# Reciprocal roots of four RMS norms: a power on GpSimd in place of a square root on ACT and a Newton step on DVE

## The chip, the cores and the metric

The kernel runs on one core of a Trainium2 chip. TensorE multiplies matrices; ACT (ScalarE) evaluates functions and casts; DVE (VectorE) does elementwise work; GpSimd (POOL) is a further elementwise engine that here sets constants only; SyncE (SP) issues nearly all DMAs. Each engine works through its own queue in order, and semaphores join them. The metric is device time in microseconds (us), the median of several executions; a lower time is better.

## What is computed

One decoder layer over 512 positions of width 1024: attention and a gated recurrence side by side, then a feed-forward block with a causal convolution. It has four RMS norms, two before a block (pre) and two behind one (post):

```python
def rms_norm(x, g):
    xf = x.astype(jnp.float32)
    y = xf * lax.rsqrt(jnp.mean(xf * xf, axis=-1, keepdims=True) + RMS_EPS)
    return (y * g.astype(jnp.float32)).astype(x.dtype)
...
h = rms_norm(x, g_pre_mix[l])
proj = h @ w_in[l]
...
mix = jnp.concatenate([attn, lru], axis=-1) @ w_out[l]
x = x + rms_norm(mix, g_post_mix[l])
h = rms_norm(x, g_pre_ffn[l])
up = causal_dwconv(h @ w_up[l], w_conv_ffn[l], b_conv_ffn[l])
c_u, c_g = jnp.split(up, 2, axis=-1)
ffn = (jax.nn.gelu(c_g, approximate=True) * c_u) @ w_down[l]
x = x + rms_norm(ffn, g_post_ffn[l])
```

Each norm needs one reciprocal root for each position. With 512 positions on 128 partitions that is a column of 128 values four times per norm, 16 roots in all.

## The kernel before

Positions are cut into four tiles of 128 (t = 0 to 3). Every fp32 operand of a matmul is split into a high and a low part (`split`, lines 83 to 85: ACT casts the high part, line 84, and DVE subtracts it, line 85), and a product is three matmuls (`mm3`, lines 77 to 81). A framework orders the instructions of all engines by the program's order and their readiness, sets the semaphores, and gives the tiles of a pool their places one behind another.

The start: SyncE loads x and the first weights; for each tile `norm_transpose` (line 135) squares x on ACT with a running sum into `ss` (line 140), takes the root (`rstd_of`, line 121), multiplies x by root and weight on DVE (line 145, tile hn), transposes on TensorE (line 151, ptr) and splits the result into hT. The first projections (px, first for half the positions) need hT of tiles 0 and 1 and a split weight. Then come the small parameters of the recurrence (line 255 on, with an Exp on ACT in line 258 and a chain of small DVE instructions), the recurrence, attention, and the output projection.

The post norms are in `wide` (line 531), which makes 512 columns at a time (n = 0, 1) of the output projection and of the down projection: `weighted` (line 506) squares the PSUM bank on ACT with a running sum (line 510), and multiplies it by the weight on DVE (line 518). For n = 0 two small DVE instructions (line 513) turn the sum into the biases for the second half; for n = 1 the root is taken. `post_norm` (line 521) multiplies by the root and adds the residual (line 526). Behind the output projection the next pre norm follows tile by tile (`mixed`, line 561), and its transposed tiles h2T feed the up projection (pup). Behind the down projection the tiles go out by DMA (line 529).

One root (`rstd_of`) is five instructions: a square root on ACT (line 125), a scaled copy of the sum on DVE (line 126), a reciprocal (line 128) and a Newton step in two DVE instructions (lines 129 and 131). Line 119 takes a root of a constant at the very start, so that ACT loads the table for Sqrt early; a function whose table is not the loaded one costs a table load on ACT.

Lines 157, 159 and 575 allocate tiles that nothing uses (shift0, shift1, shift2); they move the tiles behind them in their pools. The second activation tile of the up projection lies in a pool at the other end of the memory.

Of the kernel before, what the change touches and what calls it, by code (L numbers as in the profile page):

```python
# [12 lines left out]
F32 = mybir.dt.float32  # L13
F32R = mybir.dt.float32r
BF16 = mybir.dt.bfloat16
AF = mybir.ActivationFunctionType
ALU = mybir.AluOpType

P = 128
S = 512  # L20
D = 1024
# [15 lines left out]
EPS = 1e-6  # L37
# [15 lines left out]
def hybrid_layer(  # L53
# [6 lines left out]
    nc = tc.nc  # L60
# [3 lines left out]
    cp = ctx.enter_context(tc.tile_pool(name="cp", bufs=1))  # L64
# [5 lines left out]
    def bank(name, tag):  # L70
        return ps.tile([P, 512], F32, tag=tag, name=name, bufs=BANKS[tag])
# [11 lines left out]
    def split(h, l, src, sub=None):  # L83
        nc.scalar.copy(h, src)  # L84
        (sub or nc.vector).tensor_sub(l, src, f32(h))  # L85
# [16 lines left out]
    xres = cp.tile([P, NT, D], F32, name="xres")  # L102
# [8 lines left out]

    consts = cp.tile([P, 2], F32, name="consts")
    nc.vector.memset(consts[:, 0:1], EPS)
    nc.vector.memset(consts[:, 1:2], -EPS / 2)

    root = cp.tile([P, 1], F32, name="root")
    nc.scalar.activation(root, consts[:, 0:1], AF.Sqrt)

    def rstd_of(ss, first, name):


        v = cp.tile([P, 5], F32, tag="rs", name=name, bufs=8)
        nc.scalar.activation(v[:, 0:1], ss, AF.Sqrt, scale=1.0 / D, bias=first[:, 0:1])
        nc.vector.tensor_scalar(
            v[:, 1:2], ss, -0.5 / D, first[:, 1:2], op0=ALU.mult, op1=ALU.add)
        nc.vector.reciprocal(v[:, 2:3], v[:, 0:1])
        nc.vector.scalar_tensor_tensor(
            v[:, 3:4], v[:, 2:3], v[:, 1:2], v[:, 2:3], op0=ALU.mult, op1=ALU.mult)  # L130
        nc.vector.scalar_tensor_tensor(
            v[:, 4:5], v[:, 3:4], 1.5, v[:, 2:3], op0=ALU.add, op1=ALU.mult)
        return v[:, 4:5]

    def norm_transpose(t, g, hT, pool):

        hn = pool.tile([P, D], F32, tag="hn", name="hn", bufs=4)
        sq = pool.tile([P, D], BF16, tag="sqn", name="sqn")
        ss = cp.tile([P, 1], F32, tag="ss", name="ss", bufs=8)
        nc.scalar.activation(sq, xres[:, t], AF.Square, accum_out=ss)  # L140
        r = rstd_of(ss, consts, "rpre")
        w = D // len(g)
        for n, gn in enumerate(g):
            hs = slice(n * w, (n + 1) * w)
            nc.vector.scalar_tensor_tensor(
                hn[:, hs], xres[:, t, hs], r, gn, op0=ALU.mult, op1=ALU.mult)
        for half in range(2):
            pt = bank("ptr", "tr")
            for j in range(4):
                k = 4 * half + j  # L150
                nc.tensor.transpose(pt[:, j * P:(j + 1) * P], hn[:, k * P:(k + 1) * P], ident)
            sl = (slice(None), slice(4 * half, 4 * half + 4), slice(t * P, (t + 1) * P))
            split(hT[0][sl], hT[1][sl], pt.rearrange("p (k q) -> p k q", q=P))
# [44 lines left out]
    for t in range(NT):  # L198
        norm_transpose(t, gpre, hT, pp)
# [7 lines left out]
    for r0, src in ((0, w_conv_lru[0]), (16, b_conv_lru), (20, b_r), (24, b_i), (28, lam)):  # L207
        v = src.rearrange("a (t c) -> (a t) c", c=P)
# [85 lines left out]
    def xr_block(t):  # L294
        return split_w(raw_xr[t // 2][:, :, (t % 2) * P:(t % 2 + 1) * P], KD, P), bank("px", "mm")

    first = [xr_block(t) for t in range(2)]
# [172 lines left out]
    for n in range(-LAG, len(tiles)):  # L470
        if 0 <= n + LAG < len(tiles):
            pr, s, i = tiles[n + LAG]
# [11 lines left out]
        pr, s, i = tiles[n]  # L484
# [21 lines left out]
    def weighted(pn, n, yg, g, ss):  # L506

        hs = slice(n * 512, (n + 1) * 512)
        sq = wp.tile([P, 512], BF16, tag="sq", name="sq", bufs=1)
        nc.scalar.activation(sq, pn, AF.Square, accum_out=ss[:, n:n + 1])  # L510
        if n == 0:
            for i, f in ((2, 1.0), (3, -0.5)):
                nc.vector.tensor_scalar(
                    ss[:, i:i + 1], ss[:, 0:1], f / D, f * EPS, op0=ALU.mult, op1=ALU.add)
            r = None
        else:
            r = rstd_of(ss[:, 1:2], ss[:, 2:4], "rpost")
        nc.vector.tensor_mul(yg[:, hs], pn, g[:, hs])
        return r

# [10 lines left out]
    def wide(src, x_at, ks, n, k_last, yg, g, ss, resident, done, held_split=None):  # L531


        tags = ("mm", "mm", "mm", "av") if n == 0 else ("sc", "sc", "mm", "mm")
        py = [bank(f"py{t}", tags[t]) for t in range(NT)]

        def units(k0, k1):
            raw = load_raw(src[k0 * P:k1 * P, n * 512:(n + 1) * 512], k1 - k0, 512)
            return [(u, split_w(raw[:, u - k0:u - k0 + 2], 2, 512)) for u in range(k0, k1, 2)]

        def mms(t, k0, w):
            for j in range(2):
                mm3(py[t], x_at(k0 + j, slice(t * P, (t + 1) * P)),
                    at(w, slice(None), j), k0 + j == ks[0][0], k0 + j == k_last)

        for k0, k1 in ks[:len(ks) - resident]:
            for u, w in units(k0, k1):
                for t in range(NT):
                    mms(t, u, w)
        held = [uw for k0, k1 in ks[len(ks) - resident:] for uw in units(k0, k1)]  # L550
        if held_split:
            held_split()
        for t in range(NT):
            for u, w in held:
                mms(t, u, w)
            r = weighted(py[t], n, yg[t], g, ss[t])
            done(t, r)
# [3 lines left out]
    def mixed(t, r):  # L561
        post_norm(yg[t], r, t, False)
        norm_transpose(t, (gpre2,), h2T, np_)

    yg = [np_.tile([P, D], F32, name=f"yg{t}") for t in range(NT)]
    ss = [cp.tile([P, 4], F32, tag="ss3", name="ss3", bufs=8) for t in range(NT)]
# [84 lines left out]
    ss = [cp.tile([P, 4], F32, tag="ss3", name="ss3", bufs=8) for t in range(NT)]  # L651
# [40 lines left out]
```

## Time and profile before

| | us |
|---|---|
| median of 3 executions | 589.58 (588.92 to 589.71) |
| the profiled execution | 590.37 |
| its span, first to last instruction | 588.5 |
| TensorE busy | 571.9 |
| DVE busy | 360.0 |
| ACT busy | 278.8 |
| GpSimd busy | 2.8 |

The page of the profile gives the busy time of each engine over the span, then the span in slices, the DMA queues, the chain of work that ended last, and the costliest groups of instructions. PE is TensorE, PEld its weight loads, PEclk the clock that it was granted, as a share of full speed. Where rows come from a list in order of time, they read: start in us, length in us, engine, line, operation, result<-operands, shapes, count, and in brackets how long the engine had stood idle before and who released it. Matmuls overlap, so their spacing is read from their starts.

### The profile page before, as it was taken

The numbers are of one execution on the slowest core, as the hardware profiler recorded it, in microseconds if no ns is written. First come the engines' busy times: TensorE is split into PE (matmuls) and PEld (weight loads), VectorE is DVE, ScalarE is ACT, GpSimd is POOL, SyncE is SP. The second block draws the span as 40 slices with busy tenths as digits, with TensorE's granted clock in tenths as the row PEclk, the third lists the DMA queues.
The fourth block names the chain that finished last, engine by engine and source line by source line (L and its number), as shares of the span: only waits on it lengthen the run. The fifth ranks groups of instructions, "written<-read, shape, count | busy, mean of one in ns | idle before, by whom it ended". The sixth has DMA issues, their size and how long they took to land.

```text
span 588.5 us, 6972 instructions
## 1 busy us (share of the span) xinstructions
PE 571.9 (97%) x2704; PEld 472.7 (80%) x2704; DVE 360.0 (61%) x664; ACT 278.8 (47%) x455; POOL 2.8 (0%) x10
## 2 busy tenths in 40 slices
PE   6989999999999999999999999999999999999995
PEld 3977888777788879988888888888888888888884
DVE  5869695788996896566656656656656521241225
ACT  7538954777775772534534434443444322132121
POOL 1000000000000000000000000000000000000000
PEclk9999999999999999999999999999999999999998
DMA  7562426233110634004403403413414223332103
GB/s 234 188 216 74 143 78 196 85 107 95 41 46 5 214 105 144 1 2 142 143 15 128 144 26 117 143 40 104 144 56 144 87 73 100 91 130 72 36 1 143
DMA packets 52265, 59.62 MB, mean 101 GB/s; under 512 B 2448, under 2 KB 41568, under 8 KB 52233
## 3 DMA queue, kind: packets, MB, share of 16 engines
q1 hardware_dynamic: 51201, 57.61, 30.5%
q10 hardware_dynamic: 1032, 1.57, 0.8%
q8 instruction: 21, 0.34, 0.2%
q14 instruction: 11, 0.09, 0.0%
HBM read 57.06 MB, written 3.69 MB: 103 GB/s over the span
## 4 chain that ended last, share of the span: by engine, by line
PE 88%; DVE 5%; ACT 3%; DMA 2%; issue 1%; DVEq 0%; SPq 0%
PE pup L80 14%; PE pup L81 14%; PE pup L79 14%; PE py L81 8%; PE py L80 8%; PE py L79 8%; PE pq L79 2%; PE pq L80 2%; PE pq L81 2%; PE pav L456 2%; DMA raw<-in_w_up_dram 2%; PE px L81 1%; PE px L79 1%; PE px L80 1%; PE ptp L446 1%; PE pv L80 1%
## 5 line engine op out<-in xcount | busy, mean ns | idle before, releaser
L85 DVE TENSOR_TENSOR wl<-raw,wh 128x1024 fp32r<-128x1024 f32 x82 | 100.1, 1221 | 125.2 <-ACT wh L84 124.5
L84 ACT CAST wh<-raw 128x1024 fp32r<-128x1024 f32 x82 | 85.6, 1048 | 144.0 <-PE py L81 72.2
L80 PE MATMUL pup<-h2Tl,wh 128*128 128x512 f32 x320 | 124.5, 389 | 0.0
L81 PE MATMUL pup<-h2Th,wl 128*128 128x512 f32 x320 | 124.5, 389 | 0.0
L79 PE MATMUL pup<-h2Th,wh 128*128 128x512 f32 x320 | 124.3, 389 | 0.0
L80 PEld LDWEIGHTS pup<-h2Tl,wh 128*128 128x128 f32 x320 | 60.1, 188 | 12.5
L81 PEld LDWEIGHTS pup<-h2Th,wl 128*128 128x128 f32 x320 | 60.1, 188 | 12.5
L79 PEld LDWEIGHTS pup<-h2Th,wh 128*128 128x128 f32 x320 | 60.0, 188 | 12.2
L79 PE MATMUL py<-wh,acth 128*128 128x512 f32 x176 | 68.9, 391 | 0.0
L81 PE MATMUL py<-wh,actl 128*128 128x512 f32 x176 | 68.8, 391 | 0.0
L80 PE MATMUL py<-wl,acth 128*128 128x512 f32 x176 | 68.8, 391 | 0.0
L80 PEld LDWEIGHTS py<-wl,acth 128*128 128x128 f32 x176 | 33.1, 188 | 7.2
L81 PEld LDWEIGHTS py<-wh,actl 128*128 128x128 f32 x176 | 33.1, 188 | 7.2
L79 PEld LDWEIGHTS py<-wh,acth 128*128 128x128 f32 x176 | 33.1, 188 | 7.1
L614 DVE SCALAR_TENSOR_TENSOR yu<-pup,par,yu 128x511 f32<-128x511 f32 (+1 forms) x44 | 33.0, 749 | 4.3 <-ACT yu L612 3.5
L621 ACT ACTIVATE yg<-yg 128x512 f32<-128x512 f32 x22 | 13.9, 632 | 44.9 <-DVE yg L614 44.9
L614 DVE SCALAR_TENSOR_TENSOR yg<-pup,par,yg 128x511 f32<-128x511 f32 (+1 forms) x44 | 32.8, 746 | 2.0 <-ACT yg L612 1.2
L622 DVE TENSOR_TENSOR yu<-yu,yg 128x512 f32<-128x512 f32 x22 | 15.2, 692 | 18.3 <-ACT yg L621 18.3
L81 PE MATMUL py<-wh,mixTl 128*128 128x512 f32 x64 | 25.4, 397 | 0.0
L79 PE MATMUL pq<-hTh,wh 128*128 128x512 f32 x64 | 25.4, 396 | 0.0
L81 PE MATMUL pq<-hTh,wl 128*128 128x512 f32 x64 | 25.3, 396 | 0.0
L79 PE MATMUL py<-wh,mixTh 128*128 128x512 f32 x64 | 25.2, 395 | 0.0
(196 smaller groups left out, 938.9 us busy)
## 6 DMA issues: line engine op xcount, KB each, us to landing
raw<-in_w_up_dram SPq DMA_DIRECT2D x22, 1024.0 KB, 5.1
raw<-in_w_down_dram SPq DMA_DIRECT2D x10, 1024.0 KB, 5.0
raw<-in_w_in_dram SPq DMA_DIRECT2D x5, 1024.0 KB
rawqk<-in_w_in_dram SPq DMA_DIRECT2D x8, 512.0 KB, 5.3
raw<-in_w_out_dram SPq DMA_DIRECT2D x4, 1024.0 KB, 5.1
xres<-in_x_dram SPq DMA_DIRECT2D x4, 512.0 KB, 5.6
out_dram<-yz SPq DMA_DIRECT2D x8, 256.0 KB, 2.0
toep<-fbd ACTq DMA_DIRECT2D x1, 1536.0 KB
```

Of the source, the lines that this page charges most:

```text
L79: nc.tensor.matmul(o, lh, rh, start=start, stop=False)
L80: nc.tensor.matmul(o, lh, rl, start=False, stop=False)
L81: nc.tensor.matmul(o, ll, rh, start=False, stop=stop)
L84: nc.scalar.copy(h, src)
L85: (sub or nc.vector).tensor_sub(l, src, f32(h))
L446: nc.tensor.transpose(ptr[:, j * P:(j + 1) * P], st[:, j * P:(j + 1) * P], ident)
L456: nc.tensor.matmul(pav[:, j * P:], vs, pT[i][:, j * S:j * (S - P) + S], start=j == 0 and i == 0, stop=j == NT - 1 and i == 1)
L614: nc.vector.scalar_tensor_tensor(y[:, d:], pt[:, :S - d], w_conv_f(2 - d, blk), y[:, d:], op0=ALU.mult, op1=ALU.add)
L621: nc.scalar.activation(yg, yg, AF.Gelu_apprx_tanh)
L622: nc.vector.tensor_mul(yu, yu, yg)
```

## The change

`rstd_of` takes the square root no more. The Square on ACT scales by D to the power -0.5, so that its running sum is the mean square at once; one DVE instruction adds epsilon (or, for a post norm, epsilon and the first half's mean), and GpSimd raises it to -0.5, which is a column of constants in the tile `power`. The tiles `consts` and `root` and the early square root go; the root's own tile shrinks from five columns to two; the two small instructions for n = 0 become one.

```diff
-    consts = cp.tile([P, 2], F32, name="consts")
-    nc.vector.memset(consts[:, 0:1], EPS)
-    nc.vector.memset(consts[:, 1:2], -EPS / 2)
-
-    root = cp.tile([P, 1], F32, name="root")
-    nc.scalar.activation(root, consts[:, 0:1], AF.Sqrt)
+    MEAN = D ** -0.5
+    power = cp.tile([P, 1], F32, name="power")
+    nc.vector.memset(power, -0.5)
 
     def rstd_of(ss, first, name):
-        v = cp.tile([P, 5], F32, tag="rs", name=name, bufs=8)
-        nc.scalar.activation(v[:, 0:1], ss, AF.Sqrt, scale=1.0 / D, bias=first[:, 0:1])
-        nc.vector.tensor_scalar(
-            v[:, 1:2], ss, -0.5 / D, first[:, 1:2], op0=ALU.mult, op1=ALU.add)
-        nc.vector.reciprocal(v[:, 2:3], v[:, 0:1])
-        nc.vector.scalar_tensor_tensor(
-            v[:, 3:4], v[:, 2:3], v[:, 1:2], v[:, 2:3], op0=ALU.mult, op1=ALU.mult)
-        nc.vector.scalar_tensor_tensor(
-            v[:, 4:5], v[:, 3:4], 1.5, v[:, 2:3], op0=ALU.add, op1=ALU.mult)
-        return v[:, 4:5]
+        v = cp.tile([P, 2], F32, tag="rs", name=name, bufs=8)
+        nc.vector.tensor_scalar(v[:, 0:1], ss, first, None, op0=ALU.add)
+        nc.gpsimd.tensor_tensor(v[:, 1:2], v[:, 0:1], power, op=ALU.pow)
+        return v[:, 1:2]
...
-        nc.scalar.activation(sq, xres[:, t], AF.Square, accum_out=ss)
-        r = rstd_of(ss, consts, "rpre")
+        nc.scalar.activation(sq, xres[:, t], AF.Square, scale=MEAN, accum_out=ss)
+        r = rstd_of(ss, EPS, "rpre")
...
-        nc.scalar.activation(sq, pn, AF.Square, accum_out=ss[:, n:n + 1])
+        nc.scalar.activation(sq, pn, AF.Square, scale=MEAN, accum_out=ss[:, n:n + 1])
         if n == 0:
-            for i, f in ((2, 1.0), (3, -0.5)):
-                nc.vector.tensor_scalar(
-                    ss[:, i:i + 1], ss[:, 0:1], f / D, f * EPS, op0=ALU.mult, op1=ALU.add)
+            nc.vector.tensor_scalar(ss[:, 2:3], ss[:, 0:1], EPS, None, op0=ALU.add)
             r = None
         else:
-            r = rstd_of(ss[:, 1:2], ss[:, 2:4], "rpost")
+            r = rstd_of(ss[:, 1:2], ss[:, 2:3], "rpost")
```

## Rows read from the trace of the kernel before

**Rows 1.** The page: the span, the busy time of each engine with its share and its instructions, and one of the three groups of matmuls of the up projection.

```profile
span 588.5 us, 6972 instructions
...
PE 571.9 (97%) x2704; PEld 472.7 (80%) x2704; DVE 360.0 (61%) x664; ACT 278.8 (47%) x455; POOL 2.8 (0%) x10
...
L80 PE MATMUL pup<-h2Tl,wh 128*128 128x512 f32 x320 | 124.5, 389 | 0.0
```

**Rows 2.** Busy time of each engine in stretches of the span: the stretch, its length, then busy us (instructions) of PE, PEld, DVE, ACT and POOL, the granted clock, the DMA share and GB/s. The row that begins with "sum" adds six stretches of 6 us from 198 to 234 us.

```profile
0.00:10.00 10.00, 5.69 (x12) 2.73 (x12) 4.12 (x15) 6.35 (x12) 1.74 (x8) 1.00 0.80 278
...
40.00:50.00 10.00, 7.96 (x34) 6.04 (x33) 6.57 (x10) 5.31 (x9) 0.00 (x0) 1.00 0.49 165
...
580.00:588.50 8.50, 1.92 (x9) 1.22 (x7) 3.95 (x9) 0.98 (x3) 0.00 (x0) 0.77 0.32 123
...
sum 36.00, PE 34.84 PEld 30.36 DVE 29.53 ACT 20.31 POOL 0.00; mean PE 5.81 PEld 5.06 DVE 4.92 ACT 3.39 POOL 0.00
```

**Rows 3.** The instructions that write or read the pre norms' root, by line: shortest, median and longest in ns, first and last start in us, shapes.

```profile
L126 DVE TENSOR_SCALAR rpre<-ss,consts x8: 206/211/215, 5.7 to 228.1; 128x1 f32<-128x1 f32 x8
L125 ACT ACTIVATE rpre<-ss,consts x8: 294/296/301, 5.7 to 228.1; 128x1 f32<-128x1 f32 x8
L128 DVE RECIPROCAL rpre<-rpre x8: 152/155/164, 6.1 to 228.4; 128x1 f32<-128x1 f32 x8
L129 DVE SCALAR_TENSOR_TENSOR rpre<-rpre x8: 210/220/221, 6.3 to 228.6; 128x1 f32<-128x1 f32 x8
L131 DVE SCALAR_TENSOR_TENSOR rpre<-rpre x8: 150/156/161, 6.5 to 228.8; 128x1 f32<-128x1 f32 x8
```

**Rows 4.** All engines in order of time at the start: the end of the first tile's Square, and what DVE does for tiles 0 and 1.

```profile
5.51 0.18 ACT L140 ACTIVATION_READ_ACCUMULATOR sqn<-xres 128x1 f32 x1
5.73 0.21 DVE L126 TENSOR_SCALAR rpre<-ss,consts 128x1 f32<-128x1 f32 x1 [4.68 <-ACT sqn L140]
...
6.77 1.41 DVE L145 SCALAR_TENSOR_TENSOR hn<-xres,rpre,gpre 128x512 f32<-128x512 f32 x2
...
8.86 0.75 DVE L145 SCALAR_TENSOR_TENSOR hn<-xres,rpre,gpre 128x512 f32<-128x512 f32 x1
```

**Rows 5.** The instructions on the sums of squares: the small DVE instruction with two constants.

```profile
L513 DVE TENSOR_SCALAR ss<-ss x16: 142/145/156, 189.6 to 522.4; 128x1 f32<-128x1 f32 x16
```

**Rows 6.** GpSimd in order of time, the whole span (four of nine rows, the last of them the last).

```profile
0.34 0.11 POOL L679 MEMSET const-uint8-127<- 128x1 uint8 x1
...
0.88 0.95 POOL L181 MEMSET graw<- 128x1024 f32 x1
1.86 0.29 POOL masks.py:199 TENSOR_SCALAR_AFFINE_SELECT ident<-ident 128x128 f32<-128x128 f32 x1
...
97.59 1.10 POOL L386 MEMSET klz<- 64x512 f32 x2 [95.30 <-DVE mixTl L85]
```

**Rows 7.** DVE's groups of one shape: line, result<-operands, shapes, count, busy us, mean ns, idle before. The pre-FFN norm's product by the root.

```profile
L145 DVE SCALAR_TENSOR_TENSOR hn<-xres,rpre,gpre_ffn 128x1024 f32<-128x1024 f32 x4 | 5.1, 1280 | 0.0
```

**Rows 8.** TensorE in order of time at the start: the first of the dense matmuls.

```profile
13.97 0.58 PE L81 MATMUL px<-hTh,wl 128*128 128x256 f32 x1 [0.27 <-DVE wl L85]
```

**Rows 9.** DVE, SyncE, ACT and TensorE in order of time between 25 and 44 us, one row each.

```profile
25.92 0.17 DVE L259 TENSOR_SCALAR sp<-sp 128x4 f32<-128x4 f32 x1 [0.74 <-ACT sp L258]
...
30.49 0.37 SPq L89 DMA_DIRECT2D raw<-in_w_in_dram  x1
...
41.47 1.04 ACT L84 CAST wh<-raw 128x1024 fp32r<-128x1024 f32 x1 [3.61 <-DMA raw<-in_w_in_dram]
...
43.13 0.70 PE L79 MATMUL pg<-xsh,gwh 128*128 128x512 f32 x2 [2.04 <-issue]
```

**Rows 10.** ACT's groups: the table loads, three of seven lines with eight loads in all (the others are lines 119 and 359, Sqrt; 363, Gelu; 437, Exp).

```profile
L125 ACT ACT_TABLE_LOAD x2 | 2.6, 1283 | 0.0
...
L258 ACT ACT_TABLE_LOAD x1 | 1.3, 1283 | 0.0
...
L621 ACT ACT_TABLE_LOAD x1 | 1.3, 1283 | 1.6 <-DVE yg L614 1.6
```

**Rows 11.** ACT and TensorE in order of time in the middle: the first post-mix root, and the up projection's wait for a transposed tile.

```profile
199.05 1.28 ACT L125 ACT_TABLE_LOAD   x1
200.34 0.30 ACT L125 ACTIVATE rpost<-ss 128x1 f32<-128x1 f32 x1
...
218.40 0.39 PE L80 MATMUL pup<-h2Tl,fw00h 128*128 128x256 f32 x1 [0.40 <-DVE h2Tl L85]
```

**Rows 12.** DVE in order of time at the end: the last tile's root.

```profile
582.68 0.21 DVE L126 TENSOR_SCALAR rpost<-ss 128x1 f32<-128x1 f32 x1 [1.40 <-ACT sq L510]
582.81 0.68 DVE L518 TENSOR_TENSOR yz<-py,gpost_ffn 128x512 f32<-128x512 f32 x1
...
584.04 1.41 DVE L526 SCALAR_TENSOR_TENSOR yz<-yz,rpost,xres 128x512 f32<-128x512 f32 x2
```

**Rows 13.** TensorE in order of time in the down projection, second half of its columns: the first and the last of eleven matmuls in a row that read the first activation tile, and of thirteen that read the second.

```profile
544.70 0.39 PE L80 MATMUL py<-wl,acth 128*128 128x512 f32 x1
...
546.97 0.39 PE L81 MATMUL py<-wh,actl 128*128 128x512 f32 x1
...
563.63 0.39 PE L79 MATMUL py<-wh,acth 128*128 128x512 f32 x1
...
566.42 0.39 PE L79 MATMUL py<-wh,acth 128*128 128x512 f32 x1
```

## Prediction

> **What bounds the kernel now.** I read the page's busy times first, then the busy times in stretches of 10 us, then the chain that ended last for the two ends, then the lists of instructions in order of time around the sixteen roots. TensorE is busy for 571.9 us of 588.5 [rows 1]; the changed work is on ACT and DVE, so it counts only where TensorE stands still. The stretches show where that is [rows 2]: 10 - 5.69 = 4.31 us in the first 10 us, 2.04 us between 40 and 50 us, 36 - 34.84 = 1.16 us between 198 and 234 us (the middle, where the post-mix and pre-FFN norms are), and 8.5 - 1.92 = 6.58 us at the end. In those four places I cost the change.
>
> **The price of a root.** Before, one root is a scaled add on DVE (211 ns) beside ACT's square root (296 ns), then reciprocal, product and sum on DVE (155, 220, 156 ns) [rows 3]. At the first tile the sum of squares is there at 5.51 + 0.18 = 5.69, DVE starts at 5.73 and the normalising product at 6.77: 1.04 us for the root, handover included [rows 4]. After, it is one add on DVE (145 ns with two constants, as line 513 shows [rows 5]; 211 ns with a column operand, as line 126 does [rows 3]), a handover, GpSimd's power, a handover. I call R the time from the add's end to the consumer's start. The trace holds no power. From below: GpSimd's 128x1 memset takes 0.11 us [rows 6] and ACT hands over in 0.04 us [rows 4], so 0.11 + 2 x 0.04 = 0.2 us. From above: its longest single instruction takes 0.95 us [rows 6], and DVE's longest product by a root 1.28 us [rows 7]; if the power is as long as the one and stands behind the other, R = 2.2 us. I take a power of 0.55 us, between the select (0.29 us) and that memset [rows 6], as a power is more than a compare but works on one element per partition; with 0.05 us for each handover R = 0.65 us. GpSimd's queue holds nothing between its constants of the first microseconds and a memset at 97.59 [rows 6], so no instruction is held up behind a power; on DVE whatever follows the consumer waits with it.
>
> **The start.** The chain that ended last enters TensorE's first dense matmuls at 13.97, and what releases them is DVE [rows 8]. First tile: 5.73 + 0.145 + 0.65 = 6.53 in place of 6.77, 0.24 us won. Second tile: DVE has 8.86 - 8.18 = 0.68 us between the two tiles' products, all root [rows 4]. If its add is issued ahead of the first product (1.41 us long), the power lies wholly beside it and 0.68 us are won; if behind, 0.145 + 0.65 = 0.80 us stand there and 0.12 us are lost. I take the middle, 0.28 us. Tiles three and four feed matmuls that come when TensorE is already busy, and I cost them at nothing: their cover is the dense matmuls from 13.97 on. Start: 0.24 + 0.28 = 0.52 us; with R = 0.2 us 0.69 + 0.68 = 1.37 us, with R = 2.2 us -1.31 and -1.67 us.
>
> **Does it get past 41 us?** TensorE waits there 2.04 us for a cast on ACT that stands behind another cast, which waits 3.61 us for a weight transfer; SyncE issued that at 30.49, when a DVE split had freed its buffer [rows 9]. So what is won at the start lasts only if that issue moves as well. It does, I think: the split follows the same chain, and ahead of it lies the Exp table load, 1.28 us on ACT [rows 10], for which DVE stands 0.74 us [rows 9]. With the square root of the start gone, the first table that ACT needs is one for Square, loaded while it waits for x. Square and Tanh run under Exp's table without a load of their own (no line but those of Exp, Sqrt and Gelu has one) [rows 10], so if that first table is Exp's, the later load goes. If not, it stays. Value: 0 to 1.28 us; I take DVE's own wait, 0.74 us. Start and Exp together move 43.13 by 0.52 + 0.74 = 1.26 us. The Trainium skill (ScalarE: Activation LUTs, What ACT_TABLE_LOAD costs) gives about 2.66 us for a change of table, 1.28 us of it the load and the rest a drain. The trace shows the load alone: at 199.05 it takes 1.28 us and the square root starts at 200.34 [rows 11]. By the page this term would be up to 2.66 us; the rows decide.
>
> **The middle.** Eight roots lie between 198 and 234 us, with one Sqrt table load at 199.05 [rows 11], which goes. Their ACT and DVE work runs mostly beside held matmuls, and only 1.16 us of TensorE can be won [rows 2], 0.40 us of it at 218.40, where the up projection waits for the second tile's transpose [rows 11]. The root alone is shorter by 1.04 - 0.80 = 0.24 us, two in a row per tile, and the load 1.28 us. I take 0.5 us of the 1.16. From below, a power that waits out a DVE product (1.28 us [rows 7]) in each of two roots would cost 2 x (1.28 - 0.24) = 2.1 us, less some slack: a loss of up to 1.5 us.
>
> **The end.** The last root is bare: DVE's scaled add starts at 582.68 and the final product at 584.04, but the multiplication by the weight lies between them (582.81 to 583.49) and must be done anyway [rows 12]. After: add until 582.89, power back at 582.89 + 0.65 = 583.54, so the product starts 0.50 us earlier. It can't win more than 584.04 - 583.49 = 0.55 us, and loses from R = 1.15 us on. The Sqrt load of this stage, one of the two on line 125 [rows 10], lies beside matmuls and brings nothing.
>
> **The sum.** 0.52 + 0.74 + 0.5 + 0.50 = 2.26, say 2.3 us. The profiled execution took 590.37 us (span 588.5 and 1.9 around it), so it would take 588.1 us; it stands 0.79 us above the median of the three runs, 589.58 us, so on the median's side the forecast is 587.3 us. All ends good: 1.37 + 1.28 + 1.16 + 0.55 = 4.4 us, 585.2 us.
>
> **Rivals.** (a) The power is long, and takes the place of what it removes. At R = 1.9 us the first tile loses 1.0 us; the second wins 0.2 us (add ahead) or loses 1.4 us (behind), so 0.6 us; Exp still gives 0.74 us; the middle loses 2 x (0.145 + 1.9 - 1.04) = 2.0 us in two roots, of which the table load's end takes up about half, 1.1 us are left; the end loses 582.89 + 1.9 - 584.04 = 0.75 us: 2.7 us slower, 592.3 us. It turns from gain to loss at R of about 1.3 us, and is a measurable loss from about 1.6 us. For it: a power is software on an engine that so far fills constants only. Against it: that engine's instructions of one column take 0.1 us [rows 6]. The SBUF — State Buffer page of the Trainium skill (Who interferes with whom) has a rule that would make R long in the middle: a DVE instruction with two SBUF inputs and a GpSimd instruction that reads SBUF exclude each other for the whole instruction. No trace here shows that, as GpSimd reads nothing beside DVE work; by that rule the middle loses and the end does not, since its multiplication takes one input from PSUM. (b) What is won at the start is given back at 41 us, since the transfer lands no earlier, and the middle stays hidden: the end alone is left, 0.5 us, 589.1 us. For it: the transfer shares the queues with others and takes 41.4 - 30.5 = 10.9 us [rows 9]. (c) The tiles move. Two small tiles go and one comes ahead of nearly all others in the pool, and the pads of lines 157, 159 and 575 stay. That a place can matter, the down projection shows: with weights from the first activation tile twelve matmuls' starts lie 0.227 us apart (546.97 - 544.70 over ten), with the second, at the other end of the memory, (566.42 - 563.63) / 12 = 0.2325 us [rows 13]. Should the 3 x 320 matmuls of the up projection [rows 1] fall to that, they cost 960 x 0.0055 = 5.3 us, which with the forecast's gain of 2.3 us makes 592.6 us. Should the second tile be cured, 192 matmuls give 1.1 us. Against it: operands move together, and no row has anything to say on the new place. (d) The Exp load stays: 588.0 us, inside the forecast's range.
>
> **How the numbers follow.** The forecast with (d), between 585.2 and 588.4 us: 0.50. Better still, with (c) to the good: 0.04. (b): 0.20. (a): 0.19. (c) to the bad: 0.07. From the 0.2% that a measurement of this kernel can tell from no change (588.4 to 590.8 us), faster has 0.53 (0.01 of the forecast ends short of it), same 0.23 (with the mild part of (a)), slower 0.24. The range reaches from all ends good, 585.2 us, to (a), 592.3 us; the bad end of (c), 592.6 us, is left out.
>
> **What would show it.** Right: a power under 0.7 us and its consumer within 0.8 us of the add; table loads down from eight to five; TensorE's first dense matmul at about 13.4; the stall near 41 us ending about 1.3 us sooner; the final product about 0.5 us behind the multiplication's old place, at 583.5 by the old clock. Wrong: DVE idle ahead of lines that use the root, released by GpSimd, for over 1 us; a stall at 41 us that has grown by what the start won; starts of 512-column matmuls over 0.23 us apart in the up projection.

## The result, and the profile after

The changed kernel is slower: 596.11 us (median of four, 595.38 to 597.41) against 589.64 us (588.92 to 590.03), a ratio of 1.0108 with a 95% interval of 1.0094 to 1.0121. Its profiled execution took 596.51 us with a span of 594.7 us, which is 6.2 us more than the span of before. The forecast was 2.3 us faster, with a range up to 592.3 us.

The changed program is some ten lines shorter: the power is line 122, its add line 121, the product by the root line 135, the transposes line 141. The page (answers to [rows 1]):

```profile
span 594.7 us, 6918 instructions
...
PE 575.5 (97%) x2704; PEld 475.4 (80%) x2704; DVE 353.1 (59%) x607; ACT 271.2 (46%) x435; POOL 13.4 (2%) x26
```

DVE has 6.9 us less to do and ACT 7.6 us less, as the change says. TensorE, with the same 2704 matmuls, is busy 3.6 us longer. Either it was slower or it was granted a lower clock. The busy times by stretch tell which (answer to [rows 2]; the columns are those of that group):

```profile
10.00:20.00 10.00, 7.40 (x32) 6.49 (x32) 8.07 (x13) 6.21 (x11) 1.46 (x1) 1.00 0.72 223
40.00:50.00 10.00, 8.95 (x26) 6.80 (x27) 5.88 (x8) 5.19 (x8) 0.00 (x0) 0.66 0.17 64
198.00:234.00 36.00, 34.15 (x194) 29.17 (x192) 30.05 (x42) 20.29 (x34) 5.30 (x8) 1.00 0.41 138
```

Between 40 and 50 us the granted clock is 0.66 where it was 1.00. In the trace's record of the clock it is at the lower of its two levels (1.2 GHz) from 41.8 to 48.6 us and then full (2.4 GHz) until 591.3; before, it was full from 18.0 to 584.6 without a break. (Ahead of the record's first entry, at 18.0 us before and 21.3 us after, the rows print 1.00, but 256-column matmuls start 0.21 us apart there and 0.12 us behind it.) Inside the fall, TensorE's 512-column matmuls start 0.43 us apart in place of 0.23 (TensorE in order of time, two rows):

```profile
43.89 0.63 PE L80 MATMUL pg<-xsl,gwh 128*128 128x512 f32 x1
44.32 0.63 PE L81 MATMUL pg<-xsh,gwl 128*128 128x512 f32 x1
```

In the middle TensorE is idle for 36 - 34.15 = 1.85 us, where it was 1.16.

What became of the roots: GpSimd in order of time, two of 16 powers, and DVE around the first tiles.

```profile
5.87 0.55 POOL L122 TENSOR_TENSOR rpre<-rpre,power 128x1 f32<-128x1 f32 x1 [3.72 <-DVE rpre L121]
...
16.47 1.46 POOL L122 TENSOR_TENSOR rpre<-rpre,power 128x1 f32<-128x1 f32 x1 [6.97 <-DVE rpre L121]
```

```profile
5.63 0.15 DVE L121 TENSOR_SCALAR rpre<-ss 128x1 f32<-128x1 f32 x1 [4.62 <-ACT sqn L130]
6.46 1.41 DVE L135 SCALAR_TENSOR_TENSOR hn<-xres,rpre,gpre 128x512 f32<-128x512 f32 x2 [0.67 <-POOL rpre L122]
...
8.72 0.15 DVE L121 TENSOR_SCALAR rpre<-ss 128x1 f32<-128x1 f32 x1 [0.80 <-ACT sqn L130]
8.80 1.40 DVE L135 SCALAR_TENSOR_TENSOR hn<-xres,rpre,gpre 128x512 f32<-128x512 f32 x2
```

The root is as priced: a power of 0.55 us, and 6.46 - 5.78 = 0.68 us from the add's end to the consumer. The first tile's product starts 0.31 us sooner than in [rows 4]. So the loss must lie elsewhere. TensorE's idle times from 10 us to the end of the start, all rows with a wait:

```profile
11.36 1.97 PE L141 MATMUL ptr<-ident,hn 128*128 128x128 f32 x8 [2.13 <-DVE hTl L85]
17.58 0.58 PE L81 MATMUL px<-hTh,wl 128*128 128x256 f32 x1 [1.10 <-DVE wl L85]
40.02 0.96 PE L79 MATMUL pv<-wh,hTh 128*128 128x512 f32 x3 [1.80 <-ACT wh L84]
42.47 1.19 PE L79 MATMUL pg<-xsh,gwh 128*128 128x512 f32 x2 [1.04 <-issue]
```

The matmul that stood at 13.97 in [rows 8] stands at 17.58, and it waits for wl, the first weight's low part, which has nothing to do with a root. DVE's and SyncE's order of time shows why, first in the kernel before, then in the changed one:

```profile
12.71 1.21 DVE L85 TENSOR_TENSOR wl<-raw,wh 128x1024 fp32r<-128x1024 f32 x1
...
15.27 1.23 DVE L85 TENSOR_TENSOR wl<-raw,wh 128x1024 fp32r<-128x1024 f32 x1
16.41 1.40 DVE L145 SCALAR_TENSOR_TENSOR hn<-xres,rpre,gpre 128x512 f32<-128x512 f32 x2
...
15.59 1.32 SPq L89 DMA_DIRECT2D raw<-in_w_in_dram  x2
```

```profile
11.81 0.73 DVE L135 SCALAR_TENSOR_TENSOR hn<-xres,rpre,gpre 128x512 f32<-128x512 f32 x1
...
13.73 0.74 DVE L135 SCALAR_TENSOR_TENSOR hn<-xres,rpre,gpre 128x512 f32<-128x512 f32 x1
...
16.31 1.21 DVE L85 TENSOR_TENSOR wl<-raw,wh 128x1024 fp32r<-128x1024 f32 x1
...
23.61 1.22 DVE L85 TENSOR_TENSOR wl<-raw,wh 128x1024 fp32r<-128x1024 f32 x1
```

```profile
14.62 0.42 SPq L89 DMA_DIRECT2D raw<-in_w_in_dram  x1
15.09 0.58 SPq L492 DMA_DIRECT2D gpost_mix<-in_g_post_mix_dram  x1
...
26.45 4.38 SPq L89 DMA_DIRECT2D raw<-in_w_in_dram  x2
```

In the kernel before, DVE did the two wl at 12.71 and 15.27 and the products of tile three at 16.41. Now tile three's two products (11.81, 13.73) and the first of its two splits (15.64) go ahead of both. The order on DVE is made when the program is built, by readiness, and with the changed instructions the framework put tile three first. The second wl frees a load buffer, and so SyncE's queue is in another order too: before, two weight loads went out together from 15.59 on, now gpost_mix stands between them and the second goes out at 26.45.

To place the loss, the start of the same matmuls in both traces:

| matmul | before, us | after, us | later by |
|---|---|---|---|
| first transpose | 7.67 | 7.26 | -0.41 |
| first on wl (px) | 13.97 | 17.58 | +3.61 |
| first of the value projection (pv) | 35.95 | 40.02 | +4.07 |
| first of the gate projection (pgr) | 71.32 | 77.19 | +5.87 |
| 33rd on a weight's low part, output projection | 192.87 | 198.77 | +5.90 |
| 21st on a streamed weight, up projection | 256.92 | 263.33 | +6.41 |
| first of the down projection | 460.92 | 467.33 | +6.41 |
| last of the down projection | 581.52 | 588.12 | +6.59 |
| end of the span | 588.5 | 594.7 | +6.2 |

Nearly all is lost ahead of 77 us, half a microsecond in the middle, and 0.4 us is won back at the end.

### The profile page after: what moved, and what is told of

Read it like the earlier page. It is cut to its first block, busy times and chain, and to the rows that moved or that the text cites. A ratio compares the mean times of both kernels' runs of the same rounds, so it can differ in the third digit from the quotient of the medians.

```text
span 594.7 us, 6918 instructions
## 1 busy us (share of the span) xinstructions
PE 575.5 (97%) x2704; PEld 475.4 (80%) x2704; DVE 353.1 (59%) x607; ACT 271.2 (46%) x435; POOL 13.4 (2%) x26
## 4 chain that ended last, share of the span: by engine, by line
PE 86%; DVE 5%; ACT 3%; DMA 3%; issue 1%; POOL 1%; SPq 0%; DVEq 0%; POOLq 0%; ACTq 0%
PE pup L79 13%; PE pup L80 13%; PE pup L81 13%; PE py L80 8%; PE py L79 8%; PE py L81 8%; PE pq L79 2%; PE pq L80 2%; PE pq L81 2%; PE pav L446 2%; PE px L81 1%; DMA raw<-in_w_up_dram 1%; PE px L80 1%; PE px L79 1%; PE ptp L436 1%; PE pv L79 1%
```

## Theories and experiments

Theory A: the order. The shorter roots let the framework put tiles three and four ahead of the first weight's split; TensorE starts late, stalls near 40 us and loses its clock there. Theory B: the power itself, its handovers or its memory port, holds the kernel up. Beside them stand the prediction's rivals, above all (c), moved tiles.

### 1. The first weight's split written ahead of tile three

```
     for t in range(NT):
+        if t == 2:
+            first.append(xr_block(0))
+        if t == 2:
+            first.append(xr_block(1))
         norm_transpose(t, gpre, hT, pp)
```

> The changed kernel with the split of the first weight's two halves written ahead of the normalising of tiles three and four, so that DVE does the first low part (wl) before the products of tile three. All 16 roots are still powers. Theory A (the order: the shorter roots let tiles three and four go ahead of the first weight's split, and TensorE's dense run starts 3.6 us late): the first matmul on wl at 13.0 to 14.0 us in place of 17.58, no fall of the granted clock near 42 us, 586.5 to 588.5 us. Theory B (the power itself, its wait or its port, costs the time): nothing is taken from the powers, so 594 to 597 us.

Measured: 591.34 us, ratio 1.0025 (1.0016 to 1.0035). All powers are there and 1.3 us of the 6.5 are left (the kernel before took 590.04 beside it); the clock is full from 17.4 to 587.4 us. The first matmul on wl came at 14.94, a little later than said, but the gate projection started at 71.03, 0.3 us ahead of before. What is missing lies in the middle (+0.56 us between the output projection's mark of the table and the up projection's) and in the other runs of this kernel, which took 0.3 to 1.8 us longer than the profiled one; what that spread comes from was not looked into. The time lies above theory A's range and below theory B's.

### 2 and 3. The power in one part only

The 16 roots are made by two functions, the power and the old one, and each call names which; the early square root stays. In the second run the power is at the start alone, in the third everywhere else.

```
-        r = rstd_of(ss, consts, "rpre")
+        r = rstd_of(ss, EPS, "rpre") if new else rstd_old(ss, consts, "rpre")
```

> The changed kernel with the power for the four roots at the start only; the 12 roots after the mixer and at the end are the old ones (square root on ACT, reciprocal and Newton step on DVE), with the early square root and the Exp table load that belong to them. With these instructions the framework puts the first wl ahead of the products of tile three again. Theory A: the start is not late although its roots are powers: 588.5 to 590 us, the first matmul on wl before 14.5 us. Theory B: the start's loss of 5.9 us is the powers' there, so 595 to 597 us.

Measured: 589.12 us, ratio 0.9987 (0.9975 to 0.9998): slightly faster than before, with all four powers at the start. The first matmul on wl, said to come before 14.5 us, comes at 16.46, and yet nothing is lost. The gate projection starts at 69.65, 1.7 us sooner, as the stall of [rows 9] is gone: SyncE's queue has another order here, with the load of gpre_ffn ahead of the weight's in place of behind it; the weight's load goes out at 29.22 and ACT has cast it by 39.4.

> The changed kernel with the power for the 12 roots after the mixer and at the end only; the four at the start are the old ones. Both theories: the start as in the kernel before. Theory A: the later part alone, +0.4 in the middle and -0.4 at the end, 589 to 590 us. Theory B with a cost for every power: 592 us or more. Rival C (moved addresses slow the second half's matmuls): the places of the tiles are the old ones here, so no step of TensorE's pace.

Measured: 589.71 us, ratio 1.0001 (0.9990 to 1.0011). The middle costs 0.64 us here, the end wins 0.4. The start is not quite as before, although up to 44 us its instructions stand in the same order on SyncE, DVE and TensorE (one root's instruction moved on ACT): the weight's load goes out 0.71 us sooner than in [rows 9] and is cast 1.47 us sooner, so that the stall near 41 us is 0.85 us and the gate projection starts at 69.94, 1.38 us ahead of before.

```profile
29.78 0.37 SPq L89 DMA_DIRECT2D raw<-in_w_in_dram  x1
...
40.00 1.05 ACT L84 CAST wh<-raw 128x1024 fp32r<-128x1024 f32 x1 [2.42 <-DMA raw<-in_w_in_dram]
```

The medians of the two kernels differ by 0.3 us. So a place behind 41 us in a single trace can be off by about a microsecond, and the medians decide.

### 4. The order of after, with no power at all

The kernel before, whose two first low parts are queued on DVE as in the changed kernel: the first behind tile three's first split (the expectation says tile four's), the second behind tile four's last. issue_after orders the issue and adds no wait; done_l holds the two splits of the tile just written. Lines are left out at the dots.

```
+        with tc.issue_after(ins.ins):
+            nc.vector.tensor_sub(l, src, f32(h))
...
+        if t >= 2:
+            first.append(xr_block(t - 2, done_l[t - 2]))
```

> The kernel before, with no power in it, whose first two low parts (wl) are queued on DVE behind the first and the last hTl of tile four (with the order of issue alone, no wait more), so that DVE's order at the start is that of the changed kernel. Theory A: the start's loss comes without any power: the first matmul on wl at 17 us or later, 593 to 597 us; if the granted clock falls again near 42 us it is the late start that brings it, if not, 592 to 593.5. Theory B: 589 to 590.5 us.

Measured: 597.21 us, ratio 1.0125 (1.0108 to 1.0143). The whole loss, and not one power. TensorE's waits for wl and for pv are those of the changed kernel, and the clock is at the lower level from 41.9 to 48.7 us. TensorE in order of time, two rows:

```profile
17.97 0.58 PE L81 MATMUL px<-hTh,wl 128*128 128x256 f32 x1 [0.98 <-DVE wl L97]
...
40.78 0.97 PE L79 MATMUL pv<-wh,hTh 128*128 128x512 f32 x3 [1.80 <-ACT wh L84]
```

This run and the ninth settle that the 6 us are the order's, and not the power's.

### 5. A product in the power's place

```
-        nc.gpsimd.tensor_tensor(v[:, 1:2], v[:, 0:1], power, op=ALU.pow)
+        nc.gpsimd.tensor_tensor(v[:, 1:2], v[:, 0:1], power, op=ALU.mult)
```

> The changed kernel with GpSimd's power made a product with the same two inputs (the roots are then not computed: each norm is scaled by -0.5 times the mean square). The order of all engines stays that of the changed kernel. Theory A (the order costs the time, the power's length does not): 594 to 597 us, the granted clock falls near 42 us again. Theory B (the power's length or its port): the loss shrinks with the product's shorter time, to 592 us or less.

Measured: 593.82 us, ratio 1.0059 (1.0043 to 1.0075), between the two ranges. The product takes 0.19 us where the power took 0.55. The clock falls again (40.6 to 47.4 us) and the gate projection is 5.04 us late, so the start's loss stays, as A says. But the middle turns from +0.51 us to -1.09 us. TensorE's waits there, first in the changed kernel, then in this run:

```profile
212.16 1.09 PE L141 MATMUL ptr<-ident,hn 128*128 128x128 f32 x8 [0.54 <-DVE hn L135]
219.03 1.06 PE L141 MATMUL ptr<-ident,hn 128*128 128x128 f32 x8 [0.53 <-DVE rpost L121]
225.53 1.06 PE L141 MATMUL ptr<-ident,hn 128*128 128x128 f32 x8 [0.69 <-DVE hn L135]
234.18 1.06 PE L141 MATMUL ptr<-ident,hn 128*128 128x128 f32 x8 [0.27 <-DVE hn L135]
```

```profile
211.06 1.09 PE L141 MATMUL ptr<-ident,hn 128*128 128x128 f32 x8 [0.26 <-DVE hn L135]
223.45 1.06 PE L141 MATMUL ptr<-ident,hn 128*128 128x128 f32 x8 [0.17 <-DVE hn L135]
```

The transposes of a normalised tile stand in TensorE's queue at the same places in both; 0.54 + 0.53 + 0.69 + 0.27 = 2.03 us of waiting became 0.43. There the power's length does count, because the transposes stand where with a GpSimd instruction of 0.2 us the tile would be almost ready. In the kernel before they stood further back (the first three 45 to 69 matmuls behind their tile's last one, now 32 or 33), and waited for nothing.

### 6 and 7. One late split at a time

The fourth run's edit for the first wl alone (behind tile three's first split, not tile four's as the expectation has it), and for the second alone.

> The kernel before with the first low part (wl) alone queued behind the first hTl of tile four; the second wl stays in its place behind it, and SP's queue keeps its order. It parts theory A in two. A1 (the dense run's late start itself costs the time): the first matmul on wl at 17 us or later and most of the 6 us lost, 593 us or more. A2 (the second wl matters, because it frees the raw buffer that SP's next weight load waits for, and a late load starves TensorE near 40 us, where the clock falls): the second weight load goes out before 22 us, no stall at 38 us and no fall of the clock, 589.5 to 592 us.

Measured: 592.34 us, ratio 1.0037 (1.0025 to 1.0050), between the two ranges. The first matmul on wl is at 17.82, TensorE's full clock begins at 23.7 in place of 18.0, and the gate projection is 1.93 us late. The clock doesn't fall later.

> The kernel before with the second low part (wl) alone queued behind the last hTl of tile four; the first wl stays early. SP's second weight load then goes out after the late wl, and the load of gpost_mix moves ahead of it. A1 (the dense run's late start costs the time): it starts at 14 us here, so 589 to 591.5 us. A2 (the late release of the raw buffer and the late load): the load goes out at 24 us or later, TensorE stalls near 38 to 40 us, the clock falls near 42 us, 593 to 597 us.

Measured: 589.64 us, ratio 0.9995 (0.9984 to 1.0005). The load went out at 24.23, and ACT cast it in time (SyncE and ACT in order of time, one row each):

```profile
24.23 0.38 SPq L89 DMA_DIRECT2D raw<-in_w_in_dram  x1
```

```profile
30.66 1.05 ACT L84 CAST wh<-raw 128x1024 fp32r<-128x1024 f32 x1 [2.33 <-DMA raw<-in_w_in_dram]
```

Run 7 shares with run 4 that the first two blocks are written earlier, so that alone costs nothing. And A2 is wrong: a late load alone starves nobody. A1 explains a third: the first wl late alone costs 2.5 us in the median (592.34 against 589.82), of the 7.2 us of run 4. The full loss needs both. With both, ACT's queue has the cast that pv needs behind a convolution start (xc) that waits for the last px matmul. ACT in the kernel before, where this cast is early, and in the changed kernel:

```profile
28.15 1.04 ACT L84 CAST wh<-raw 128x1024 fp32r<-128x1024 f32 x1
```

```profile
38.25 0.78 ACT L300 ACTIVATE xc<-px,par 128x512 f32<-128x512 f32 x1 [4.69 <-PE px L81]
38.93 2.93 ACT L84 CAST wh<-raw 128x1024 fp32r<-128x1024 f32 x3
```

### 8. Power at the start and at the end

> The changed kernel with the power at the start (four roots) and after the down-projection (four roots), and the old roots for the eight between. If the middle's roots lose 0.5 to 0.6 us by their place in TensorE's queue and the end's gain 0.4 us, it is the run with the power at the start alone less 0.4: 588.7 us, 0.9978 of the kernel before. Theory B (each power costs): above that run's 589.1 us.

Measured: 589.00 us, ratio 0.9978 (0.9968 to 0.9988). As said: faster than both kernels. The last matmul is 1.36 us ahead of before and the span 1.8 us shorter, so the end gives 0.4 us. Most of its lead comes, as in run 2, from the stall near 41 us, which is gone.

### 9. A useless square root

```
+    eps_t = cp.tile([P, 1], F32, name="eps_t")
+    nc.vector.memset(eps_t, EPS)
+    root = cp.tile([P, 1], F32, name="root")
+    nc.scalar.activation(root, eps_t, AF.Sqrt)
 
     MEAN = D ** -0.5
```

> The changed kernel, all 16 roots powers, with nothing added but the early square root on a constant that the kernel before had (its result is used by nobody). It brings a square-root table load and the Exp table load back: work that was removed. With these instructions the framework puts the first two wl ahead of the products of tile three again. Theory A (the order costs the time): 588.6 to 590.4 us, that is the run with the power at the start alone plus 0.6 for the middle, less 0.4 at the end; no fall of the clock near 42 us. Theory B: work added to the changed kernel makes it no faster, 596 to 598 us.

Measured: 589.43 us, ratio 0.9998 (0.9987 to 1.0009). Work that nobody uses, with a table load of 1.28 us that comes back, makes the changed kernel 6.7 us faster. DVE does the first split early again (the second at 16.82 is behind tile three's products, not ahead of them as said), and ACT has pv's cast at 29.33. TensorE has no idle time between 40 and 50 us, though much between 10 and 20 us:

```profile
11.19 1.23 DVE L85 TENSOR_TENSOR wl<-raw,wh 128x1024 fp32r<-128x1024 f32 x1 [1.32 <-ACT wh L84]
13.53 1.40 DVE L140 SCALAR_TENSOR_TENSOR hn<-xres,rpre,gpre 128x512 f32<-128x512 f32 x2
16.82 1.22 DVE L85 TENSOR_TENSOR wl<-raw,wh 128x1024 fp32r<-128x1024 f32 x1
...
29.33 1.05 ACT L84 CAST wh<-raw 128x1024 fp32r<-128x1024 f32 x1 [0.64 <-ACT wh L84]
```

```profile
10.00:20.00 10.00, 6.39 (x30) 5.77 (x31) 7.56 (x12) 7.20 (x11) 1.97 (x2) 1.00 0.66 161
...
40.00:50.00 10.00, 10.00 (x44) 8.00 (x44) 7.41 (x11) 5.99 (x10) 0.00 (x0) 1.00 0.47 165
```

One part of theory A does not hold. TensorE is idle for 3.61 us between 10 and 20 us here, against 2.60 in the changed kernel, and the first matmul on wl comes at 17.43, as late as there (17.58). The first pv matmul is 1.60 us later than before (37.55), but the gate projection is 0.71 us ahead: the stall near 41 us, 2.04 us before and none here, took up what the start lost. So a late first matmul on wl does not by itself cost the 6 us. The changed kernel differs from this run by the late second wl (23.61), pv's cast behind xc, the waits near 40 us and the clock's fall.

The four powers of the start are the same in both, and in run 2, so the shorter roots alone do not make the late order either. Which of the removed instructions tips it is not shown.

### 10 and 11. The middle's transposes further back

On top of run 9 the transposes are emitted apart from the norm, and those of the first two tiles are queued behind a later matmul of the output projection.

```
+                if t >= 2 and i == 2 and len(turns) > 0:
+                    turns.pop(0)(m)
```

The transposes go behind the matmul m; the eleventh run has `i == 1`.

> The run with the square root back, and in the middle the transposes of the first two tiles queued on TensorE nine and ten matmuls later (2.0 to 2.3 us), behind a named matmul of the out-projection. If the middle's loss is TensorE waiting for the products (0.5 to 0.8 us ahead of each of four groups of transposes) because they stand too early in its queue for a power of 0.55 us, the first two waits go: 1.0 to 1.6 us less than with the square root back alone, 587.4 to 589 us. If the loss is in the powers or in DVE, no change: 589 to 590 us.

Measured: 589.54 us, ratio 0.9993 (0.9983 to 1.0003), not below 589 us as said. The two waits went, but the up projection now waits 0.80 and 0.60 us for the tiles that were transposed later. The middle costs +0.33 us, as in run 9 (+0.39).

> As the run before it, with the transposes of the first two tiles only three and four matmuls later (0.7 and 0.9 us), just over the waits of 0.5 to 0.8 us that they are to cover. If those waits are all there is to gain, it comes out as with nine and ten, 587.4 to 589 us; if later stages hang on the transposes, this one is the better by some tenths.

Measured: 588.65 us, ratio 0.9982 (0.9971 to 0.9992). The middle is at -0.35 us, so 0.7 us are won with three and four matmuls that nine and ten don't win; the 1.0 us expected of the waits came in part. With all 16 roots a power, this one too beats both kernels. Between this run and the eighth, one can't choose: their intervals overlap.

### 12. One stall taken away

In the changed kernel, ACT's cast for pv is queued ahead of xc.

```
+            cast = nc.scalar.copy(h0, raw_v[:, 0:2])
...
+        with tc.issue_after(cast.ins) if t == 2 else ExitStack():
+            nc.scalar.activation(c, px, AF.Identity, scale=w_conv_l(3, t), bias=col(16 + t))
```

> The changed kernel as it is (first two wl still late), but with ACT's high part of the value projection's first weight (wh, for pv) queued ahead of the third convolution start (xc) near 38 us, where in the changed kernel it stands behind it and TensorE waits 1.80 us for it. Refined theory (the late split loses about 2.4 us by itself, and the stalls of 1.80 and 1.04 us between 38 and 42.5 us drop the granted clock to half for 6.8 us, some 3.4 us more): the first matmul on wl stays at 17 us or later, the 1.80 us and the fall of the clock go, 590.3 to 592.5 us. Rival (the clock falls because of the late start itself): it falls near 42 us again, 594 to 596 us.

Measured: 594.86 us, ratio 1.0077 (1.0059 to 1.0096). The wait of 1.80 us went, and 1.3 us of the loss with it (596.11 to 594.86), but the next weight's cast made one of 1.12 us at 40.82, and the clock fell all the same, from 43.0 to 46.4 us, and once more from 19.1 to 22.6. The number is the rival's; its reason, that the late start drops the clock near 42 us, does not hold either, since runs 6 and 9 started as late and did not lose it. In the kernel before, a stall of 2.04 us at 41 us [rows 9] left the clock alone. What decides the fall stays open; these runs show only that it came in the four with the first wl at 16 us or later and the second at 23 us or later (after, 4, 5 and 12) and in no other.

## Why the prediction was wrong

The step that failed is this: "Tiles three and four feed matmuls that come when TensorE is already busy, and I cost them at nothing: their cover is the dense matmuls from 13.97 on." The cover is not fixed. Those matmuls need wl from the same DVE queue, and in the changed program tile three's products stand ahead of wl in it. The prediction read the trace's order as given, and asked of each step only how long it takes. Runs 4 and 9 show that the order alone loses and gives back the 6 us: run 4 loses 7.2 us without a power, run 9 nothing with all 16. How the late order costs that much is in part open: the waits near 40 us and the clock's fall came in each run that lost 4 us or more (the changed kernel, 4, 5 and 12), pv's late cast in all of these but run 12, and what sets off the fall was not found.

Point by point:

- The price of a root was right: 0.55 us and R = 0.68 us (0.65 said). That the power fell on the mark is luck, as 0.55 us was a choice between 0.29 and 0.95. Two of 16 powers took 1.46 us, both beside a wl on DVE. The rule of the Trainium skill that the prediction weighed (SBUF — State Buffer, Who interferes with whom) fits: both powers end 0.4 us behind a subtraction with two SBUF operands that began just ahead of them (16.31, 222.43), and no other power met such an instruction. A power of 1.9 us, rival (a), did not come.
- The start: first tile 0.31 us (0.24 said), of which 0.10 us is no gain of the root, as the add itself starts sooner (5.63 against 5.73); second tile 8.86 to 8.80, 0.06 us (0.28 said). DVE's queue has the third tile's add, which waits 0.80 us for ACT until 8.72, ahead of the second tile's product.
- The Exp table load went, and two others of the eight. The 0.74 us that it was to be worth past 41 us were not seen. In run 1, where the order is mended, SyncE issues that load 0.84 us sooner than in [rows 9], and ACT's cast starts only 0.32 us sooner (SyncE and ACT in order of time, one row each):

```profile
29.65 0.37 SPq L89 DMA_DIRECT2D raw<-in_w_in_dram  x1
```

```profile
41.15 1.04 ACT L84 CAST wh<-raw 128x1024 fp32r<-128x1024 f32 x1 [3.48 <-DMA raw<-in_w_in_dram]
```

  From issue to cast that is 11.50 us, against 10.98 in [rows 9] and 10.22 in run 3: this time varies by more than the term. So it is not shown that the load's earlier issue is worth nothing, as rival (b) has it, only that it did not come through in run 1; that the transfer shares its time with the 1.5 MB that ACT's queue sends from 28 us on was not tested. The stall went altogether only where SyncE's queue had another order (runs 2 and 7 to 11).
- The middle: +0.5 us in place of -0.5. The sign hangs on where the transposes stand in TensorE's queue (runs 5, 10 and 11).
- The end: 0.4 us (0.50 said), in each run with the power there. The last product starts 0.81 us behind the multiplication by the weight, where it was 1.23 [rows 12]:

```profile
589.45 0.68 DVE L506 TENSOR_TENSOR yz<-py,gpost_ffn 128x512 f32<-128x512 f32 x1
589.68 0.55 POOL L122 TENSOR_TENSOR rpost<-rpost,power 128x1 f32<-128x1 f32 x1 [3.65 <-DVE rpost L121]
590.26 1.42 DVE L514 SCALAR_TENSOR_TENSOR yz<-yz,rpost,xres 128x512 f32<-128x512 f32 x2
```

- Rival (c): the up projection kept its pace (from its 21st matmul on a streamed weight to the down projection 204.0 us before and after). The starts of the down projection's 528 matmuls span 120.79 us in place of 120.60; that is all that moved tiles may have cost.

The loss ahead of 77 us, 5.87 us, adds up from the rows. The first pv matmul is 4.07 us later than before: 1.80 us is its wait for the cast, 2.27 us the late start. The stall behind it is 1.04 us in place of 2.04, which gives 1.00 us back. From 42.47 to 48.59 us, 14 matmuls at the lower clock take 6.12 us; at 0.227 us each they would take 3.18, so the clock costs 2.9 us, an estimate. The sum is 4.07 - 1.00 + 2.9 = 5.97 us.

## What to carry to other kernels

Where a framework orders the engines, a change in the number or length of small instructions is a change of every queue; compare the order of the instructions on each engine, before any durations, around the first dense work of each stage. A late start is not yet a loss: a wait for a transfer further on may take it up, as in run 9. A gain or loss of one per cent that comes with such a change may belong to the order: pin the order, or bring it about without the change, before crediting or blaming the instruction. A shortened step helps only as far as its consumer's place in its queue suits it, and here three and four matmuls further back (588.65 us) were better than none (589.43) and than nine and ten (589.54).

## What was not expected of the hardware

A GpSimd power on 128 x 1 takes 0.55 us and a product 0.19 us; beside a DVE subtraction with two operands in SBUF of 1.2 us the same two take 1.46 and 1.10 us. The granted clock fell to half for 6.8 us (changed kernel) and 3.4 us (run 12) in the middle of a run, around waits of 1.80 and 1.04 us, and of 1.12 and 0.55 us; one of 2.04 us left it full [rows 9].
